# Gram matrices gathered head by head, three output tiles begun early, and the gate's first copy in another pool

## The chip, the cores and the metric

The kernel runs on one core of one Trainium2 chip. The metric is the time of one execution in microseconds (us), as the device reports it; several executions give a median. A core has a matrix engine (TensorE, in the profile PE, with its weight loads as PEld), three engines for element-wise work (VectorE or DVE, ScalarE or ACT, GpSimd or POOL) and SyncE (SP), which here only issues transfers. POOL issues transfers too. Each engine runs its own instructions strictly in order and waits on semaphores for the others. SBUF is the on-chip memory, PSUM the banks into which PE accumulates.

## The reference

One layer of a bidirectional encoder over two groups of 256 tokens (together T = 512 columns), model width 2048, in float32:

```
h = h + W_out [ NA(heads 0..7) ; GatedDeltaNet-bidir(heads 0..7) ]( RMSNorm(h) )
h = h + SwiGLU( RMSNorm(h) )
y = RMSNorm(h)
```

NA is neighbourhood attention on a grid. The gated DeltaNet takes q, k and v through a convolution over five tokens and a SiLU, normalises q and k, and then works in chunks of 64 tokens: for each head, chunk and direction it needs the products of keys with keys and of queries with keys (the Gram matrices), each scaled by decays, the inverse of a unit triangular 64x64 matrix made of them, and a recurrence over the chunks:

```
a_mat = where(strict, (k_beta k^T) * decay, 0)
t_mat = solve_triangular(I + a_mat, I)
u = t_mat v_beta ;  w = t_mat (k_beta * exp(g)) ;  qk = where(tri, (q k^T) * decay, 0)
v_new = u_i - w_i S ;  o = (q_i exp(g_i)) S + qk_i v_new ;  S = S exp(g_last) + (k_i ...)^T v_new
```

## The kernel before

Every large product is done in float32 by splitting each operand into a high part that PE takes at full rate and the rest: hi·hi + lo·hi + hi·lo, three matmuls (`mm3`). A weight tile of 1024x128 comes by one 512-KB transfer on SP (`w_raw`), ACT makes `w_hi` from it and DVE `w_lo` (L128 and L129). Raw, hi and lo have three buffers each. A half tile (`half_gemm`) is 24 such matmuls into a PSUM bank `ps_g` (three banks), a `col_tile` two half tiles, 128 output columns for all tokens.

PE's matmuls keep the order in which the program writes them. Everything else is put in order on its engine when the kernel is built, by a list scheduler with priorities that reckons durations; its result is a fixed row of instructions for each engine. Small jobs are written as generators (`chains`, `side`, `vector_work`) that `pump()` moves on by a step between matmuls, so the constants KQ_GAP, NA_START, LANE_START, CORE_START say after how many steps a job's matmuls or first instructions follow.

The order of the work:

1. The input is split. Then come the key and query tiles of the eight DeltaNet heads, two `col_tile`s a head. Each is evacuated (`ev_xi`), convolved (`conv_silu`: ACT `cacc`, four steps on DVE at L333, ACT `kq` with SiLU at L337; `cacc` has one buffer, `kq` two) and stored to `s_kq` by POOL. ACT squares the queries (`q_sq`, L571) and splits the squares (`sqh`; `sql` on DVE). `kq_post` (L343) follows eight steps later: 8 Gram matmuls of 64 rows and a row of ones against `sqh` and `sql` on PE, in three banks `ps_s`; ACT copies them to SBUF (`gs` L361, `qrow` L369), POOL stores them to the DRAM arrays `s_gram` (four transfers of 64 KB) and `s_qq`. `gs` uses the memory of the attention's `ev_kT` and `ev_vT`. ACT makes the decays (`E`, 22 short instructions a head) in between.
2. The eight attention heads, three `col_tile`s each (q, k, v): `qT`, `ev_kT` and `ev_vT` (L289) evacuate them, then PE transposes `ev_vT`, takes the scores, and so on. Beside them `lanes()` (L455) does the triangular inverses on DVE, all heads, chunks and directions at once, one in each partition. It begins with two transfers of 2 MB on POOL which bring all of `s_gram` into `kkq`, one for each direction, and eight small ones for `qq`. The first DVE instruction that reads them is `nkx` (L472).
3. The value and gate tiles of the DeltaNet and the recurrences (`recur` L691, `finish_head`), whose query operand `qg` is loaded by SP.
4. The output projection: first the 16 tiles' attention half (`w_out[i, 0]`) added to the input in SBUF (`h1`) and stored to `s_h1` by POOL, then the DeltaNet half (`w_out[i, 1]`, from L870 on), with `s_h1` loaded again. The last head's recurrence runs beside the first half. The pools `dr`, `na`, `wk`, `xp` close between the halves, and `st` and `gA` open.
5. The gate and up products in blocks of seven (operands `XC`), the first of which copies its first product with ACT into `p1` (`plus_both`, L916, L917), the down projection and the last norm.

Of the kernel before, what the change touches and what calls it, by code (L numbers as in the profile page):

```python
# [8 lines left out]
F32 = mybir.dt.float32  # L9
# [9 lines left out]
P = 128  # L19
# [19 lines left out]
AHEAD = 120  # L39
NA_START = 5  # L40
NA_GAP = 10
# [3 lines left out]
CORE_START = 2  # L45
CORE_START0 = 6
LANE_START = 4
N_GAP = 1
# [15 lines left out]
def hybrid_encoder(ctx: ExitStack, tc: tile.TileContext, xT, w_in, w_ba, w_out, w_gate,  # L64
# [110 lines left out]
    def pump():  # L175
        advance(chains)
        advance(side)

    def pause(n):
        for _ in range(n):  # L180
            yield

    def half_gemm(ps, src, xs, start, stop, every=2):

        wh, wl = load_w(src, [8, P])
        for k in range(8):
# [154 lines left out]
    na = na_cm.__enter__()  # L341

    def kq_post(h, kq, sqh, sql):  # L343
        yield from pause(KQ_START if h == 0 else KQ_GAP)
# [23 lines left out]
        for pp in range(2):  # L368
            nc.scalar.copy(ranged(qrow[:1], pp), q5[:, :, pp])  # L369
        nc.gpsimd.dma_start(s_qq[h], qrow[:1])  # L370
        if h == H - 1:
            vector_work.append(lanes())

# [81 lines left out]
    def lanes():  # L455
        beta, kd, eg, dg, E = (gt[n] for n in ("beta", "kd", "eg", "dg", "E"))
        qq = vec("qq")
        for d in range(2):
            nc.gpsimd.dma_start(kkq[half[d]].rearrange("p s w c -> p (s w c)"),
                                s_gram.rearrange("k n s w c -> (k n) (s w c)"))  # L460
        for d in range(2):
# [233 lines left out]
    def recur(h, zs):  # L695
        dr = state["dr"]
        while h not in prepared:
            yield
        yield from pause(CORE_START0 if h == 0 else CORE_START)
        uq, kq, vn, kd = prepared[h]  # L700
# [148 lines left out]
    for i in pairs:  # L849
        ps = pg.tile([P, T], F32, tag="g", name="ps_g")  # L850
        half_gemm(ps, w_out[i, 0], nas, True, True, 1)
        hk = h1[i // 8][:, i % 8]
        tt(hk, hk, ps, ALU.add)
        nc.gpsimd.dma_start(s_h1[i], hk)
    while chains or side:
        pump()
    dr_cm.__exit__(None, None, None)
    na_cm.__exit__(None, None, None)
    wk_cm.__exit__(None, None, None)
    xp_cm.__exit__(None, None, None)  # L860
# [6 lines left out]
    gA = ga_cm.__enter__()  # L867
    st_cm = tc.tile_pool(name="st", bufs=1, side="right", reuse_waits="tile")
    st = st_cm.__enter__()
    acc = gA.tile([P, T], F32, tag="acc", name="ssq_acc2")  # L870
    A11, S3, S1, A12, S2, S4, A22 = range(7)
    for n, i in enumerate(pairs):
        j = i % 8
        ps = pg.tile([P, T], F32, tag="g", name="ps_g")
        hk = st.tile([P, T], F32, tag="hk", bufs=2, name="hk")
        nc.sync.dma_start(hk, s_h1[i])
        half_gemm(ps, w_out[i, 1], dns, True, True)
        tt(hk, hk, ps, ALU.add)
        nc.gpsimd.dma_start(s_h2[i], hk)
# [55 lines left out]
    def block(src, f, pool, new_out, opened=None):  # L935
# [61 lines left out]
        a = out.rearrange("p (f b) t -> p f (b t)", f=2)  # L997
        tt(a, a, rstd2[:, None, :].broadcast_to([P, 2, T]), ALU.mult)
        return out

    rstd2 = gA.tile([P, T], F32, tag="rstd2", name="rstd2")

    def token_rstd2():
        ps = sm_tile()
        mm(ps, ones, acc, start=True, stop=True)
        rstd_bcast(ps, rstd2, state["fp"], 1, "p7")

# [216 lines left out]
```

## Time and profile before

| | |
|---|---|
| median of three runs | 2338.06 us (2337.35 to 2338.17) |
| the profiled execution | 2341.7 us |
| its span, first to last instruction | 2339.9 us |
| mean granted clock of TensorE | 0.993 |
| PE busy | 2305.3 us, 99% of the span |
| DVE, ACT, POOL busy | 1614.1, 973.5, 220.5 us |
| moved by the DMA engines | 374.23 MB, mean 160 GB/s |

A row of the profile names the line, the engine, the operation, the tile that it writes and those that it reads, and how often. "Idle before, releaser" is the time that the engine stood still ahead of it and what ended this. Several views are used: what an engine waited for, an engine's timeline, windows of the span with the granted clock, and one tile's instructions.

### The profile page before, as it was taken

How to read it: one execution, taken by the hardware profiler on the slowest of the kernel's cores; microseconds unless marked ns; L12 is line 12 of the kernel's file. 1: busy time of each engine (PE TensorE's matmuls, PEld its weight loads, DVE VectorE, ACT ScalarE, POOL GpSimd, SP SyncE). 2: the span in 40 equal slices, each digit the busy share in tenths (PEclk: the TensorE clock that was granted, in tenths of full speed). 3: DMA queues.
4: the chain of work that ended last, by engine and by line, in shares of the span. 5: the costliest groups of instructions: out<-in, count | busy, mean ns of one | idle time of the engine just before them, and what ended most of it. 6: DMA issues, size and time to landing. Idle time of an engine off the chain costs nothing.

```text
span 2339.9 us, 31301 instructions
## 1 busy us (share of the span) xinstructions
PE 2305.3 (99%) x12092; PEld 1934.0 (83%) x12092; DVE 1614.1 (69%) x2380; ACT 973.5 (42%) x1472; POOL 220.5 (9%) x332
## 2 busy tenths in 40 slices
PE   9999999999999999999999999999999999999998
PEld 7887778887778788888888888888888878888887
DVE  7744699984666536788888888888888753422346
ACT  6777232333333315544444444444444331311125
POOL 2211200011000011101001001010100200000000
PEclk9999999999999999999999999999999999999999
DMA  5434623346434555677777777777776652423231
GB/s 202 133 118 140 156 93 97 102 110 201 128 118 135 198 181 182 198 197 207 198 201 203 198 201 195 208 198 207 195 193 180 216 195 94 135 99 97 92 126 73
DMA packets 105492, 374.23 MB, mean 160 GB/s; under 512 B 13840, under 2 KB 14256, under 8 KB 104192
## 3 DMA queue, kind: packets, MB, share of 16 engines
q1 hardware_dynamic: 75248, 268.74, 34.4%
q0 software_dynamic: 30096, 103.50, 19.7%
q8 instruction: 95, 1.56, 0.3%
q14 instruction: 53, 0.43, 0.1%
HBM read 336.19 MB, written 36.00 MB: 159 GB/s over the span
## 4 chain that ended last, share of the span: by engine, by line
PE 76%; DVE 12%; ACT 4%; DMA 4%; issue 3%; POOL 0%; SPq 0%; DVEq 0%; ACTq 0%; POOLq 0%
PE ps_g L76 28%; PE ps_a L76 11%; PE ps_d L76 10%; PE ps_c L76 10%; PE ps_s L76 10%; PE ps_b L76 5%; DVE w_lo L129 2%; DVE W L544 2%; DMA w_raw<-in_w_in_dram 2%; DVE prod L542 2%; DMA raw_a<-s_act 1%; ACT w_hi L128 1%; DVE cacc L333 1%; PE ps_o L76 1%; ACT E L450 1%
## 5 line engine op out<-in xcount | busy, mean ns | idle before, releaser
L129 DVE TENSOR_TENSOR w_lo<-w_raw,w_hi 128x1024 fp32r<-128x1024 f32 x222 | 271.2, 1222 | 302.2 <-ACT w_hi L128 298.8
L128 ACT ACTIVATE w_hi<-w_raw 128x1024 fp32r<-128x1024 f32 x222 | 234.2, 1057 | 538.1 <-PE ps_s L76 285.8
L76 PE MATMUL ps_g<-xhi,w_hi 128*128 128x512 f32 x896 | 362.2, 404 | 3.7 <-ACT w_hi L128 2.3
L76 PE MATMUL ps_g<-xlo,w_hi 128*128 128x512 f32 x896 | 350.5, 391 | 0.7 <-DVE xlo L237 0.7
L76 PE MATMUL ps_g<-xhi,w_lo 128*128 128x512 f32 x896 | 350.5, 391 | 0.5 <-DVE w_lo L129 0.5
L76 PE MATMUL ps_a<-xc,w_hi 128*128 128x512 f32 x704 | 252.3, 397 | 3.2 <-DVE p L917 2.1
L76 PE MATMUL ps_c<-xc,w_hi 128*128 128x512 f32 x704 | 249.1, 393 | 0.0
L76 PE MATMUL ps_d<-xc,w_hi 128*128 128x512 f32 x704 | 249.1, 393 | 0.0
L128 ACT ACTIVATE w_hi<-w_first 128x1024 fp32r<-128x1024 f32 x132 | 140.1, 1061 | 203.7 <-PE ps_c L76 108.9
L128 ACT ACTIVATE w_hi<-b 128x1024 fp32r<-128x1024 f32 x132 | 140.1, 1062 | 190.2 <-issue 111.5
L129 DVE TENSOR_TENSOR w_lo<-w_first,w_hi 128x1024 fp32r<-128x1024 f32 x132 | 161.6, 1224 | 72.2 <-ACT w_hi L128 68.1
L76 PEld LDWEIGHTS ps_g<-xhi,w_hi 128*128 128x128 f32 x896 | 168.7, 188 | 41.2 <-issue 5.7
L76 PEld LDWEIGHTS ps_g<-xhi,w_lo 128*128 128x128 f32 x896 | 168.6, 188 | 37.6 <-DVE w_lo L129 1.5
L76 PE MATMUL ps_a<-xc,w_lo 128*128 128x256 f32 x704 | 197.9, 281 | 0.0
L76 PEld LDWEIGHTS ps_g<-xlo,w_hi 128*128 128x128 f32 x896 | 169.0, 189 | 34.7 <-DVE xlo L237 1.8
L76 PE MATMUL ps_c<-xc,w_lo 128*128 128x256 f32 x704 | 197.2, 280 | 0.0
L76 PE MATMUL ps_d<-xc,w_lo 128*128 128x256 f32 x704 | 197.1, 280 | 0.0
L129 DVE TENSOR_TENSOR w_lo<-b,w_hi 128x1024 fp32r<-128x1024 f32 x132 | 161.2, 1221 | 7.5 <-ACT w_hi L128 0.9
L76 PEld LDWEIGHTS ps_a<-xc,w_hi 128*128 128x128 f32 x704 | 132.6, 188 | 39.1 <-issue 6.3
L76 PEld LDWEIGHTS ps_c<-xc,w_hi 128*128 128x128 f32 x704 | 131.8, 187 | 30.0
L76 PEld LDWEIGHTS ps_d<-xc,w_hi 128*128 128x128 f32 x704 | 131.8, 187 | 30.0
L76 PEld LDWEIGHTS ps_a<-xc,w_lo 128*128 128x128 f32 x704 | 133.7, 190 | 0.0
(332 smaller groups left out, 4309.2 us busy)
## 6 DMA issues: line engine op xcount, KB each, us to landing
w_raw<-in_w_in_dram SPq DMA_DIRECT2D x110, 512.0 KB, 3.4
w_raw<-in_w_down_dram SPq DMA_DIRECT2D x88, 512.0 KB, 3.4
b<-in_w_gate_dram SPq DMA_DIRECT2D x66, 512.0 KB, 4.1
b<-in_w_up_dram SPq DMA_DIRECT2D x66, 512.0 KB, 5.5
w_raw<-in_w_out_dram SPq DMA_DIRECT2D x32, 512.0 KB, 3.6
w_second<-in_w_gate_dram SPq DMA_DIRECT2D x22, 512.0 KB, 8.4
w_first<-in_w_gate_dram SPq DMA_DIRECT2D x22, 512.0 KB, 6.2
w_second<-in_w_gate_dram POOLq DMA_DIRECT2D x22, 512.0 KB, 5.5
```

What stands on the lines that cost most here:

```text
L76: pin(nc.tensor.matmul(*a, **k))
L128: act(out=hi, in_=src, func=AF.Copy)
L129: tt(lo, src, r32(hi), ALU.subtract)
L333: stt(a3[:, :, lo:hi], x3[:, :, lo + o:hi + o], cw[:, ct, j:j + 1], a3[:, :, lo:hi], ALU.mult, ALU.add)
L450: pin(act(out=E[half[0], s, s:], in_=G[half[0], s:], func=AF.Exp, bias=NG[half[0], s:s + 1]))
L542: tt(pv, W[:, s0:s1, s0:c], kkq[:, c, 0, None, s0:c].broadcast_to([P, n, j]), ALU.mult)
L544: nc.vector.tensor_reduce(W[:, s0:s1, c], pv, AX.X, ALU.add)
```

## The change

It has four parts.

First, the gather. The two 2-MB transfers of `lanes()` are replaced by `gather(h)`: eight transfers on POOL, each of two partitions by 8192 numbers (64 KB), that bring one head's Gram matrices into `kkq`. `kq_post` of head h calls it for head h − 1, behind its own stores, and that of head 7 for head 7 too. The loads of `qq` stay where they were. With it LANE_START goes from 4 to 2, NA_START from 5 to 8, and CORE_START0 (6, the first recurrence's pause) is dropped for CORE_START (2).

Second, three tiles of the projection's second half (EARLY) do seven of their eight steps ahead of the closing of the pools, and the eighth behind it. For the first two of them `h1` is taken from SBUF, not through `s_h1`. `st` opens earlier.

Third, `p1` comes from the pool `gA` in place of `fp`.

Fourth, `rstd2` takes the memory of `acc` in `gA`, which makes room for it.

```diff
-NA_START = 5
+NA_START = 8
...
-CORE_START0 = 6
-LANE_START = 4
+LANE_START = 2
+
+EARLY = 3
...
+    def gather(h):
+
+        for d in range(2):
+            for k in range(4):
+                p0 = d * 64 + k * 16 + h * NB
+                nc.gpsimd.dma_start(kkq[p0:p0 + NB].rearrange("p s w c -> p (s w c)"),
+                                    s_gram[k, h * NB:h * NB + NB].rearrange("n s w c -> n (s w c)"))
...
         nc.gpsimd.dma_start(s_qq[h], qrow[:1])
+        if h:
+            gather(h - 1)
         if h == H - 1:
+            gather(h)
             vector_work.append(lanes())
...
-        for d in range(2):
-            nc.gpsimd.dma_start(kkq[half[d]].rearrange("p s w c -> p (s w c)"),
-                                s_gram.rearrange("k n s w c -> (k n) (s w c)"))
...
-        yield from pause(CORE_START0 if h == 0 else CORE_START)
+        yield from pause(CORE_START)
...
-        nc.gpsimd.dma_start(s_h1[i], hk)
+        if i not in pairs[:2]:
+            nc.gpsimd.dma_start(s_h1[i], hk)
+
+    early = []
+    for i in pairs[:EARLY]:
+        ps = pg.tile([P, T], F32, tag="g", name="ps_g")
+        wh, wl = load_w(w_out[i, 1], [8, P])
+        for k in range(7):
+            while k not in finished:
+                pump()
+            mm3(ps, wh[:, k], wl[:, k], dns[k][0], dns[k][1], k == 0, False)
+            pump()
+        early.append((ps, wh, wl))
     while chains or side:
         pump()
     dr_cm.__exit__(None, None, None)
     na_cm.__exit__(None, None, None)
+    st_cm = tc.tile_pool(name="st", bufs=1, side="right", reuse_waits="tile")
+    st = st_cm.__enter__()
+    hks = []
+    for i, (ps, wh, wl) in zip(pairs[:2], early):
+        mm3(ps, wh[:, 7], wl[:, 7], dns[7][0], dns[7][1], False, True)
+        hk = st.tile([P, T], F32, tag="hk", bufs=2, name="hk")
+        tt(hk, h1[i // 8][:, i % 8], ps, ALU.add)
+        hks.append(hk)
...
-        p1 = fp.tile([P, L], F32, tag="p1", name="p1")
+        p1 = gA.tile([P, L], F32, tag="p1", name="p1")
```

The scheduler builds other rows from this. Three places follow. In the changed kernel the line numbers are one higher from the split on (w_hi L129, w_lo L130), and more further down.

ACT in the stretch of the key and query tiles, before: the weight splits, the table load and the SiLU of head 7's key tile, then of its query tile, the squares and their split.

```order
L128 ACTIVATE w_hi<-w_raw 128x1024
L337 ACT_TABLE_LOAD
L337 ACTIVATE kq<-cacc 128x2x128 x2
L128 ACTIVATE w_hi<-w_raw 128x1024
L327 ACTIVATE cacc<-ev_xi,cw 128x512
L337 ACTIVATE kq<-cacc 128x2x128 x2
L128 ACTIVATE w_hi<-w_raw 128x1024
L571 ACTIVATE q_sq<-kq 128x512
L128 ACTIVATE sqh<-q_sq 128x512
```

The same piece of the changed kernel (head 7; heads 5 and 6 have the same piece, with one `cacc` more):

```order
L129 ACTIVATE w_hi<-w_raw 128x1024 x4
L338 ACT_TABLE_LOAD
L338 ACTIVATE kq<-cacc 128x2x128 x2
L370 COPY gs<-ps_s 128x256 x2
L328 ACTIVATE cacc<-ev_xi,cw 128x512
L378 COPY qrow<-ps_s 1x2x2x64
L378 COPY qrow<-ps_s 1x2x128
L338 ACTIVATE kq<-cacc 128x2x128 x2
L580 ACTIVATE q_sq<-kq 128x512
L129 ACTIVATE sqh<-q_sq 128x512
```

Four weight splits now stand ahead of the table load, and the Gram copies `gs` of the head before have come from ahead of them to behind them.

DVE at the first attention head, before: the weight splits two by two between the evacuations of the key and the value tile.

```order
L129 TENSOR_TENSOR w_lo<-w_raw,w_hi 128x1024 x2
L289 TENSOR_TENSOR ev_kT<-ps_g,rstd 128x512
L129 TENSOR_TENSOR w_lo<-w_raw,w_hi 128x1024 x2
L289 TENSOR_TENSOR ev_vT<-ps_g,rstd 128x512
L129 TENSOR_TENSOR w_lo<-w_raw,w_hi 128x1024 x2
L604 TENSOR_TENSOR na_s<-ps_s,bias 128x512
```

The changed kernel from the end of the key and query tiles on: six splits, the key tile, and then the lanes (`nkx` and what follows).

```order
L647 SCALAR_TENSOR_TENSOR qT<-ps_g,rstd 128x512
L130 TENSOR_TENSOR w_lo<-w_raw,w_hi 128x1024 x6
L290 TENSOR_TENSOR ev_kT<-ps_g,rstd 128x512
L481 TENSOR_SCALAR nkx<-kkq 128x64
L156 TENSOR_SCALAR nw<-nkx 128x64
L512 TENSOR_TENSOR kkq<-kkq,E 128x32x64
```

The piece 28 rows further on, with the evacuation of the value tile in it:

```order
L504 TENSOR_TENSOR Dm<-nkr,rb 128x64
L483 TENSOR_TENSOR nqs<-nqx,nqr 128x64
L290 TENSOR_TENSOR ev_vT<-ps_g,rstd 128x512
L493 TENSOR_SCALAR rqd<-nqr 128x64 x2
L505 TENSOR_SCALAR ndm<-Dm 128x64
```

`ev_vT` stood two weight splits behind `ev_kT`; now 34 instructions of the lanes stand between them, from `nkx` to `nqs`.

SP at the start of the output projection, before: `nml` are the attention outputs, `h_0` and `h_1` the input (512 KB each), `qg` the last head's queries.

```order
L838 DMA nml<-s_na 128x2x512 x4
L136 DMA w_raw<-in_w_out_dram 128x1024
L842 DMA h_1_6601<-in_xT_dram 128x1024
L842 DMA h_0_6600<-in_xT_dram 128x1024 x4
L842 DMA h_1_6601<-in_xT_dram 128x1024 x3
L702 DMA qg<-s_eg 128x2048
```

The changed kernel:

```order
L847 DMA nml<-s_na 128x2x512 x4
L137 DMA w_raw<-in_w_out_dram 128x1024
L711 DMA qg<-s_eg 128x2048
L851 DMA h_0_6697<-in_xT_dram 128x1024 x4
L851 DMA h_1_6698<-in_xT_dram 128x1024 x4
```

`qg` has moved from behind the eight loads to ahead of them.

More of the change, by code (lines that the diff above doesn't have):

```diff
@@ L867, in hybrid_encoder @@
     gA = ga_cm.__enter__()
-    st_cm = tc.tile_pool(name="st", bufs=1, side="right", reuse_waits="tile")
-    st = st_cm.__enter__()
     acc = gA.tile([P, T], F32, tag="acc", name="ssq_acc2")
@@ L873, in hybrid_encoder @@
         j = i % 8
[L874 to L878, printed above, removed]
+        if n < 2:
+            hk = hks[n]
+        else:
+            hk = st.tile([P, T], F32, tag="hk", bufs=2, name="hk")
+            nc.sync.dma_start(hk, s_h1[i])
+            if n < EARLY:
+                ps, wh, wl = early[n]
+                mm3(ps, wh[:, 7], wl[:, 7], dns[7][0], dns[7][1], False, True)
+            else:
+                ps = pg.tile([P, T], F32, tag="g", name="ps_g")
+                half_gemm(ps, w_out[i, 1], dns, True, True)
+            tt(hk, hk, ps, ALU.add)
         nc.gpsimd.dma_start(s_h2[i], hk)
@@ L997, in block @@
         a = out.rearrange("p (f b) t -> p f (b t)", f=2)
-        tt(a, a, rstd2[:, None, :].broadcast_to([P, 2, T]), ALU.mult)
+        tt(a, a, state["rstd2"][:, None, :].broadcast_to([P, 2, T]), ALU.mult)
         return out
-    rstd2 = gA.tile([P, T], F32, tag="rstd2", name="rstd2")
     def token_rstd2():
@@ L1005, in token_rstd2 @@
         mm(ps, ones, acc, start=True, stop=True)
-        rstd_bcast(ps, rstd2, state["fp"], 1, "p7")
+        state["rstd2"] = gA.tile([P, T], F32, tag="acc", name="rstd2")
+        rstd_bcast(ps, state["rstd2"], state["fp"], 1, "p7")
     def open_gate():
```

## The prediction

> **What bounds the kernel now.** The page comes first. It tells which engine fills the span.
>
> ```profile
> span 2339.9 us, 31301 instructions
> PE 2305.3 (99%) x12092; PEld 1934.0 (83%) x12092; DVE 1614.1 (69%) x2380; ACT 973.5 (42%) x1472; POOL 220.5 (9%) x332
> ```
>
> TensorE (PE) works 2305.3 of 2339.9 us. There are some 35 us that it does not fill, and a change that leaves the matmuls as they are can win no more than a part of these. It can lose without limit: anything that makes PE wait goes straight into the time. So the question for each edit is whether a PE wait goes or comes. The second view is what PE waits for, over the whole span (total, times, longest, in us):
>
> ```profile
> PE ps_g L76 <- ACT w_hi L128: 4.1, 2, 2.3
> PE ps_s L76 <- DVE qg L739: 3.1, 1, 3.1
> PE ps_a L76 <- DVE p L917: 2.1, 1, 2.1
> PE ps_s L79 <- DVE ev_vT L289: 1.8, 2, 1.4
> ```
>
> Three of these lie where the change works. The third view is PE's timeline at those places (start, duration, matmul, and in brackets the idle time ahead of it), and the fourth the windows around them (window, its length, busy us of PE, PEld, DVE, ACT and POOL, granted clock, DMA share, GB/s):
>
> ```profile
> 259.45 0.50 PE L76 MATMUL ps_g<-xhi,w_hi 128*128 128x512 f32 x1 [2.27 <-ACT w_hi L128]
> 260.71 0.56 PE L76 MATMUL ps_g<-xhi,w_lo 128*128 128x512 f32 x1 [0.52 <-DVE w_lo L129]
> ```
>
> ```profile
> 257.00:268.00 11.00, 8.20 (x30) 6.09 (x29) 8.54 (x17) 6.33 (x16) 1.06 (x2) 0.84 0.53 173
> 783.00:795.00 12.00, 8.94 (x55) 6.63 (x56) 6.67 (x17) 1.66 (x4) 0.57 (x1) 0.72 0.45 162
> 968.00:988.00 20.00, 17.92 (x89) 14.82 (x88) 15.29 (x19) 11.07 (x16) 3.24 (x4) 0.91 0.82 217
> ```
>
> A PE gap costs more than its idle time: behind each of the three the granted clock drops. 11 us at 0.84 lack 1.8 us, 12 us at 0.72 lack 3.4 us (some of it inside the gap), 20 us at 0.91 lack 1.8 us.
>
> **What the change takes away.** Each gap is priced as idle time plus clock.
>
> The first, at 257 us, has its cause in the old gather: of five weight loads between 228 and 262 us one took 24.3 us to land, because the two 2-MB transfers of kkq held the DMA engines (the tile views of w_raw and of kkq in that stretch, then POOL's timeline):
>
> ```profile
> DMA to landing us min/median/max: 3.3/20.1/24.3
> ```
>
> ```profile
> DMA to landing us min/median/max: 14.2/19.3/24.5
> ```
>
> ```profile
> 233.04 1.05 POOL L459 DMA_DIRECT2D kkq<-s_gram  x2 [4.13 <-DMA s_gram<-gs]
> ```
>
> With the 4 MB cut into 64 pieces over eight heads that burst is gone: 2.27 + 0.52 + 1.8 = 4.5 us. The second, at 785 us, is the last head's query load, which stood behind eight 512-KB loads on SP; the order now has it ahead of them. Its tile's view:
>
> ```profile
> L702 SPq DMA_DIRECT2D qg<-s_eg x1: 326/326/326, 777.1 to 777.1; - x1
> DMA to landing us min/median/max: 8.9/8.9/8.9
> ```
>
>  That gives 3.1 us of idle and 2.4 of the 3.4 of clock: 5.5 us (3.1 to 6.4). The third, at 979 us: p1 took its place in a pool that had to wait for the last reader of the pool before it; in gA it doesn't, and ACT's copy stands ahead of the weight work. 2.1 + 1.8 = 3.8 us. Together 13.8 us.
>
> By the Trainium skill ("TensorE: Matmul & The Clock Gate", section "HAM oscillation — how this bites in real kernels") only idle gaps above some 3.4 us throttle PE; here a gap of 2.08 us was followed by a drop to 0.91 over 20 us, so the row decides; by the rule the three gaps would be worth 7.9 us and the forecast would lie 6 us higher.
>
> **What it moves, and what that costs.** The order of the changed kernel shows more than the diff says. From head 4 on, ACT's stream has the weight splits w_hi in blocks of four, and the silu of both tiles of a head (kq), the Gram copies of the head before (gs) and the convolution's first product (cacc) all behind such a block. Before, they stood one by one between single w_hi. The reason is the gathers: POOL issues eight of them ahead of each head's store of kq, and the scheduler reckons that kq's buffer comes free late. How late it really comes free no longer matters, since ACT runs in order and the fourth w_hi of the block has a wait of its own: three buffers, so it starts when PE has ended the half tile three before. The trace shows this wait, and the length of a half tile (24 matmuls), in the distance of two rows: 238.47 − 233.03 = 5.44 us, 0.227 us for each matmul.
>
> ```profile
> 206.87 1.28 ACT L337 ACT_TABLE_LOAD   x1 [1.73 <-issue]
> 208.16 0.73 ACT L337 ACTIVATE kq<-cacc 128x256 f32<-128x256 f32 x2
> 209.74 0.71 ACT L327 ACTIVATE cacc<-ev_xi,cw 128x512 f32<-128x512 f32 x1
> 214.20 0.72 ACT L337 ACTIVATE kq<-cacc 128x256 f32<-128x256 f32 x2 [3.75 <-DVE cacc L333]
> 215.78 0.61 ACT L571 ACTIVATE q_sq<-kq 128x512 f32<-128x512 f32 x1
> 216.43 0.63 ACT L128 ACTIVATE sqh<-q_sq 128x512 fp32r<-128x512 f32 x1
> 225.33 0.63 ACT L361 COPY gs<-ps_s 128x256 f32<-128x256 f32 x2
> 233.03 1.06 ACT L128 ACTIVATE w_hi<-w_raw 128x1024 fp32r<-128x1024 f32 x1 [4.37 <-PE ps_g L76]
> 238.47 1.06 ACT L128 ACTIVATE w_hi<-w_raw 128x1024 fp32r<-128x1024 f32 x1 [4.38 <-PE ps_g L76]
> ```
>
> ```profile
> 211.01 3.10 DVE L333 SCALAR_TENSOR_TENSOR cacc<-ev_xi,cw,cacc 128x508 f32<-128x508 f32 x4
> 217.09 0.69 DVE L129 TENSOR_TENSOR sql<-q_sq,sqh 128x512 fp32r<-128x512 f32 x1
> 232.50 0.69 DVE L289 TENSOR_TENSOR ev_kT<-ps_g,rstd 128x512 f32<-128x512 f32 x1 [3.82 <-DMA s_gram<-gs]
> ```
>
> Heads 5, 6 and 7. Let T be the end on PE of the half tile for which the block's last w_hi waits. From there the chain is w_hi 1.06, table 1.28, k's kq 0.73, gs 0.63, q's cacc 0.71, four DVE steps 3.10, q's kq 0.72: 8.2 us. PE's order puts this head's Gram matmuls six matmuls into the next half tile, 6 × 0.227 = 1.4 us behind T. So PE stands still for 6.8 us. Then come the two row matmuls: 0.61 + 0.71 + 0.63 = 1.95 us to sqh and 2.8 to sql against some 1.1 us of Gram matmuls and a row matmul between, so 1.3 us more; before, the two rows took 0.5:
>
> ```profile
> 215.84 1.09 PE L76 MATMUL ps_s<-kq 128*64 128x128 f32 x16
> 217.11 0.39 PE L76 MATMUL ps_s<-sqh,ones_r 128*1 128x512 f32 x1 [0.18 <-ACT sqh L128]
> 217.83 0.40 PE L76 MATMUL ps_s<-sql,ones_r 128*1 128x512 f32 x1 [0.34 <-DVE sql L129]
> ```
>
> That is 6.8 + 1.3 − 0.5 = 7.6 us of idle for a head. The clock behind it I put between the 1.8 and the 3.4 us of the windows, at 2.4: 10 us a head, 30 us for three (23 without any clock, 33 with the whole). Head 4 only finds its PSUM buffers late, since gs of head 3 stands behind a w_hi: 1.5 us (0 to 3).
>
> The first attention head. Now DVE has six w_lo in one piece ahead of ev_kT, the evacuation of its k tile, and ACT six w_hi ahead of gs of head 7. PE needs the k tile's PSUM bank when it has ended the half tile for which the sixth w_hi waits: call that U. gs ends at U + 1.06 + 0.63 = U + 1.7. ev_kT takes gs's place in memory and so waits for the stores of s_gram; before, it started 232.50 − 225.96 = 6.5 us behind the end of gs. That makes U + 8.2, and U + 8.9 for its end: 8.9 us of idle where there was none, and 1 us of clock, as little work follows before the next wait: 9.9 us.
>
> That next wait is for ev_vT. In DVE's order 34 operations of the lanes have moved ahead of it, beginning with nkx, which needs all the gathers. POOL issues s_gram from U + 1.7:
>
> ```profile
> 225.98 2.42 POOL L363 DMA_DIRECT2D s_gram<-gs  x4 [10.18 <-ACT gs L361]
> 228.40 0.51 POOL L370 DMA_DIRECT2D s_qq<-qrow  x1
> 234.08 2.88 POOL L464 DMA_DIRECT2D qq<-s_qq  x6
> 247.50 0.48 POOL L464 DMA_DIRECT2D qq<-s_qq  x1 [10.54 <-DMA kkq<-s_gram]
> ```
>
> 2.42 + 0.51 bring it to U + 4.6, and 16 gathers follow at 1.05 / 2 = 0.53. The last two rows show that a ninth transfer (here behind two of kkq and six of qq) waits for the landing of the first, so the second eight wait for the first eight. For the landing of a 64-KB gather there is no row; the nearest is that of s_gram's tile, whose stores have the same bytes:
>
> ```profile
> DMA to landing us min/median/max: 2.1/4.8/24.5
> ```
>
> (This row is of tile s_gram and counts the two big ones as well.) With its 4.8 us: first eight landed from U + 9.9, second eight issued by U + 14.1, all landed at U + 18.9. The bounds: 16 us if no landing holds the issue and one 32-KB row takes 24.5 / 8 = 3.1 us (the old gather's 128 rows over 16 engines), and 54 us if all rows go through the same two engines (16 × 3.1 behind U + 4.6). I take 19.
>
> ```profile
> 262.49 0.21 DVE L472 TENSOR_SCALAR nkx<-kkq 128x64 f32<-128x64 f32 x1
> 265.68 1.22 DVE L129 TENSOR_TENSOR w_lo<-w_raw,w_hi 128x1024 fp32r<-128x1024 f32 x1
> 274.71 0.23 DVE L474 TENSOR_TENSOR nqs<-nqx,nqr 128x64 f32<-128x64 f32 x1
> ```
>
> From nkx to the end of nqs before: 12.4 us, with two w_lo (2.4) and about 1 us of attention steps inside that now stand elsewhere, and without one product of some 1 us that now stands here: 10 us. (The eight loads of qq stand behind the gathers on POOL, each behind the landing of the eighth transfer ahead of it, and would land some 5 us after the gathers; DVE asks for them, at nqx, some 5 us after nkx, so that costs nothing, or a us or two.) With 0.69 for itself ev_vT ends at U + 29.7. PE reaches its transposes six matmuls behind U + 8.9, at U + 10.3: 19.4 us idle, and 2.4 of clock: 21.8 us. Behind that I see no further PE wait: the next weight split stands some 12 us of DVE work later, and PE has two half tiles in hand.
>
> Early tiles of the output projection: head 7 is finished when they begin, so nothing waits for it, but all three weight buffers stay taken until each tile's last matmuls, so the fourth tile's w_hi (1.06) starts at the first tile's end, and its w_lo (1.22) follows when DVE has made two additions of 0.69: 1.4 + 1.2 = 2.6 us against eight matmuls, 1.8 us, so 1 us (0 to 3). The rest (SBUF copies of two tiles, rstd2 in acc's place, the earlier recurrence) lies beside PE work of 5.44 us a half tile and costs nothing; if that cover failed, it would be a DVE step of 0.69 us.
>
> **The sum.** Lost: 30 + 1.5 + 9.9 + 21.8 + 1 = 64. Won: 13.8. Net +50. The profiled execution took 2341.7 us, so 2392 by its own time; the median lies 3.6 us lower, so 2388.
>
> **Rivals.** (a) The other side: the stalls don't come, since the rows moved behind the blocks are done before PE asks. The deciding point is the cover of 1.4 us against a chain of 8.2; for it speaks only that ACT is 42% busy over the span, against it the row of w_hi released by PE. Then only the gaps go: 2338 − 14 = 2324. It would turn at stalls of 14 us in all.
> (b) The gathers fall on few DMA engines. Then nkx comes up to 35 us later (54 − 19): 2423; with four engines about half of it, 2400. For it speaks that two partitions are two rows; against it nothing in the profile, which has no such transfer. The Trainium skill ("DMA: Bandwidth & Descriptors", section "Why a DMA increments its semaphore by 16 and not by 1") lets such a GpSimd transfer use two engines, taken in turn by a cursor, which would speak against this rival; no run here shows it yet.
> (c) The stalls come, but at their lower ends: 23 for the three heads, none for head 4, 8.9, and 16.4 for the vT wait, no clock: 48 − 14 = +34, 2372.
> (d) The stalls and the gains balance: within 0.2% (4.7 us, about what a measurement of this kernel can tell from no change), 2338.
>
> Chances: forecast 0.57, (b) 0.15, (c) 0.13, (a) 0.12, (d) 0.03. Faster 0.12, same 0.03, slower 0.85. The range leaves out (a), (d) and a little of each end: 2352, some 20 us under (c), which a smaller vT wait alone would give, to 2424, the end of (b).
>
> **What would show it.** PE's timeline between 150 and 240 us with three waits of 6 to 8 us ahead of ps_s<-kq; then one of some 9 us ahead of ps_g, released by ev_kT, and one of some 19 us ahead of ps_s<-ident,ev_vT; no gap ahead of S,qg near the output projection and of ps_a near the gate's start; granted clock below 1 behind each stall. The forecast is wrong if PE has no gap over 3 us in that stretch, or if a gap of tens of us has a weight load (DMA) as its releaser.

## The result, and the profile after

The changed kernel takes 2403.7 us in the median (2402.7 to 2406.3, six runs) where the kernel before, run beside it, takes 2338.1 us (2337.3 to 2340.5, six runs). The ratio is 1.028 (1.0267 to 1.0293): 65.6 us slower. In the two profiled executions the span grew from 2339.9 to 2400.9 us, by 61.0. The page of the changed kernel begins:

```profile
span 2400.9 us, 31348 instructions
PE 2306.8 (96%) x12092; PEld 1934.7 (81%) x12092; DVE 1616.0 (67%) x2380; ACT 977.6 (41%) x1474; POOL 250.2 (10%) x392
PEclk9998879999999999999999999999999999999999
```

PE is busy as long as before (2306.8 against 2305.3 us) and does as many matmuls, so the 61 us are waiting. The row of clocks says where: slices 4 to 6, 180 to 360 us, the key and query tiles and the first attention head. PE's waits in the changed kernel (total, times, longest, in us):

```profile
PE ps_s L80 <- DVE ev_vT L290: 34.6, 1, 34.6
PE ps_s L77 <- ACT kq L338: 20.6, 3, 7.8
PE ps_s L77 <- ACT gs L370: 10.1, 1, 10.1
PE ps_g L77 <- DVE ev_kT L290: 7.0, 1, 7.0
...
PE ps_a L77 <- DVE p L951: 1.2, 1, 1.2
...
PE ps_d L77 <- ACT w_hi L129: 1.1, 1, 1.1
...
PE ps_g L77 <- DVE w_lo L130: 0.8, 1, 0.8
```

Six single waits are new and large. PE's timeline puts them in order (start, duration, matmul, idle time ahead of it and releaser): heads 4 to 7, then the first attention head's key and value tiles.

```profile
154.88 1.33 PE L77 MATMUL ps_s<-kq 128*64 128x128 f32 x10 [10.11 <-ACT gs L370]
...
187.62 1.12 PE L77 MATMUL ps_s<-kq 128*64 128x128 f32 x8 [7.80 <-ACT kq L338]
...
219.93 1.34 PE L77 MATMUL ps_s<-kq 128*64 128x128 f32 x10 [6.40 <-ACT kq L338]
...
253.09 1.32 PE L77 MATMUL ps_s<-kq 128*64 128x128 f32 x9 [6.39 <-ACT kq L338]
...
294.96 0.79 PE L77 MATMUL ps_g<-xhi,w_hi 128*128 128x512 f32 x1 [7.03 <-DVE ev_kT L290]
...
332.47 0.87 PE L80 MATMUL ps_s<-ident,ev_vT 128*128 128x128 f32 x3 [34.59 <-DVE ev_vT L290]
```

Together they are 72.3 us. They pull the clock down too, as the windows around one stall of a head, the long wait and the matmuls behind it show:

```profile
212.00:228.00 16.00, 9.20 (x40) 6.63 (x39) 8.42 (x11) 13.01 (x30) 7.47 (x14) 0.68 0.32 97
...
301.50:335.70 34.20, 3.23 (x10) 2.81 (x11) 14.16 (x42) 0.58 (x1) 11.88 (x24) 0.50 0.08 28
335.70:345.00 9.30, 9.30 (x42) 7.69 (x42) 9.19 (x12) 3.94 (x11) 1.43 (x2) 1.00 0.12 31
```

The matmuls that ran at half clock behind the six waits lost 12.4 us (half of 3.3, 4.7, 6.5, 4.0, 3.1 and 3.2 us). The account against before: lost 72.3 + 0.8 (the early tile's w_lo) + 12.4 = 85.5; gone are 13.6 us of smaller idle times and 9.6 of clock behind four of them, 23.2. That makes 62.3, where 61.0 were measured.

What went, and what of it stayed away: the gap of 2.27 + 0.52 us at 259 us (4.5 with its clock); the 3.06 at 788 us (5.9 with clock); of 2.08 at 981 us two gaps of 1.10 and 1.20 are left, without a drop of the clock (1.5); three gaps of 1.59, 1.38 and 0.87 around 310, 446 and 544 us (3.8); and one in the down projection, 1.81 + 0.72 at 1905 us (5.9 with clock).

### The profile page after: what moved, and what is told of

The parts are those of the page before. It is cut to its first block, busy times and chain, and to the rows that moved or that the text cites. A ratio compares the mean times of both kernels' runs of the same rounds, so it can differ in the third digit from the quotient of the medians.

```text
span 2400.9 us, 31348 instructions
## 1 busy us (share of the span) xinstructions
PE 2306.8 (96%) x12092; PEld 1934.7 (81%) x12092; DVE 1616.0 (67%) x2380; ACT 977.6 (41%) x1474; POOL 250.2 (10%) x392
## 4 chain that ended last, share of the span: by engine, by line
PE 89%; DVE 4%; ACT 3%; DMA 2%; issue 1%; SPq 0%; POOL 0%; DVEq 0%; ACTq 0%
PE ps_g L77 39%; PE ps_s L77 12%; PE ps_a L77 10%; PE ps_c L77 10%; PE ps_d L77 10%; PE ps_b L77 5%; DVE cacc L334 1%; PE ps_o L77 1%; DMA kkq<-s_gram 1%; PE ps_s L80 1%; DVE w_lo L130 1%; DMA w_raw<-in_w_in_dram 1%; ACT w_hi L129 1%; ACT E L462 0%; ACT E L464 0%
## 5 line engine op out<-in xcount | busy, mean ns | idle before, releaser
L130 DVE TENSOR_TENSOR w_lo<-w_raw,w_hi 128x1024 fp32r<-128x1024 f32 x222 | 271.1, 1222 | 309.4 <-ACT w_hi L129 306.1
L129 ACT ACTIVATE w_hi<-w_raw 128x1024 fp32r<-128x1024 f32 x222 | 234.4, 1057 | 579.3 <-PE ps_s L77 280.7
L129 ACT ACTIVATE w_hi<-w_first 128x1024 fp32r<-128x1024 f32 x132 | 140.1, 1061 | 204.3 <-PE ps_c L77 109.2
L129 ACT ACTIVATE w_hi<-b 128x1024 fp32r<-128x1024 f32 x132 | 140.2, 1062 | 193.0 <-issue 115.4
L130 DVE TENSOR_TENSOR w_lo<-w_first,w_hi 128x1024 fp32r<-128x1024 f32 x132 | 161.7, 1225 | 75.0 <-ACT w_hi L129 70.9
L130 DVE TENSOR_TENSOR w_lo<-b,w_hi 128x1024 fp32r<-128x1024 f32 x132 | 161.2, 1221 | 7.7 <-ACT w_hi L129 0.8
```

The lines of the kernel that those rows point to most:

```text
L129: act(out=hi, in_=src, func=AF.Copy)
L130: tt(lo, src, r32(hi), ALU.subtract)
```

## The experiments

Two theories stood at the start. **A**: there are two causes. The gathers ahead of each store of `kq` in POOL's queue make the scheduler build the blocks on ACT and DVE, and with them the waits at heads 4 to 7 and at `ev_kT`; LANE_START = 2 puts the lanes ahead of `ev_vT`, and with it the sixth wait. **B**: the gathers' slow landing is the cause of the waits, the constants do little. The later runs ask how much of each wait is a loss of its own. Every kernel computes the whole layer. Medians, with before beside it on the same chip:

| run | kernel | us | before | ratio (95%) |
|---|---|---|---|---|
| e1 | gathers alone | 2395.1 | 2336.4 | 1.025 (1.0233–1.0267) |
| e2 | LANE_START 2 alone | 2351.9 | 2336.4 | 1.0068 (1.0053–1.0083) |
| e3 | changed, LANE_START 4 | 2391.7 | 2336.4 | 1.0236 (1.0221–1.0251) |
| e4 | early tiles, p1, rstd2 alone | 2337.5 | 2336.4 | 1.0006 (0.9996–1.0015) |
| e5 | gathers alone, on SP | 2397.0 | 2334.6 | 1.026 (1.0246–1.0274) |
| e6 | gathers alone, in two halves | 2377.3 | 2334.6 | 1.0178 (1.0164–1.0192) |
| e7 | changed, one-row gathers | 2404.2 | 2334.6 | 1.0293 (1.0279–1.0307) |
| e8 | CORE_START0 2, p1 alone | 2336.2 | 2334.6 | 1.0002 (0.9993–1.0011) |
| e9 | e1, stores on SP | 2356.9 | 2338.0 | 1.0076 (1.0063–1.0089) |
| e10 | changed, stores on SP | 2350.0 | 2338.0 | 1.0049 (1.0034–1.0065) |
| e11 | e10, LANE_START 4 | 2350.0 | 2338.0 | 1.0043 (1.003–1.0056) |
| e12 | e9, CORE_START0 2, p1 | 2359.5 | 2338.0 | 1.0086 (1.0073–1.0099) |

### Gathers alone (e1_gather_only)

The kernel before with the gather part of the change, the constants as before.

```diff
         nc.gpsimd.dma_start(s_qq[h], qrow[:1])
+        if h:
+            gather(h - 1)
         if h == H - 1:
+            gather(h)
             vector_work.append(lanes())
```

> The kernel before, with the new gathers alone (all constants, the early tiles and p1 as before). Theory A (order): the loss comes from where the gathers on POOL make the scheduler put the SiLU, the Gram copies and ev_kT behind blocks of weight splits; the wait for ev_vT does not come from the gathers but from LANE_START, which has its old value here. So the four waits ahead of ps_s<-kq stay (10.1 + 7.8 + 6.4 + 6.4 us and some 8 us of clock), one wait of 7 to 10 us at the first attention head stays, the 34.6 us wait goes, and the old gap at 257 us (4.5 us) goes: about 2380 us. Theory B (transfers): the loss comes from the gathers themselves, slow and late, and the whole of it stays, the ev_vT wait too: about 2415 us.

It took 2395 us, between the 2380 of A and the 2415 of B. PE's waits:

```profile
PE ps_s L76 <- ACT kq L337: 19.2, 3, 6.4
PE ps_s L76 <- ACT gs L369: 10.1, 1, 10.1
PE ps_s L76 <- DMA uq<-s_uq: 9.4, 2, 8.7
PE ps_s L79 <- DVE ev_vT L289: 7.4, 2, 7.1
PE ps_g L76 <- DVE ev_kT L289: 7.2, 1, 7.2
```

The four waits at the heads and one at an evacuation are there with nothing but the gathers: that half of A holds. The wait of 34.6 us is not there, as A has it. But two waits stand in its place that A did not have: 7.2 us for a second `ev_kT`, which now stands behind the lanes, and 8.7 us at the first recurrence, far later, for `uq`, which the lanes make.

### LANE_START alone (e2_lanes2)

```diff
-LANE_START = 4
+LANE_START = 2
```

> The kernel before with one digit changed, LANE_START 2 for 4; gathers, early tiles and p1 as before. Theory A (order): DVE's row now has the lanes' first 34 instructions ahead of ev_vT, although no transfer is changed. nkx waits for the 2-MB gathers (landed at 258 us), ev_vT ends some 11 us later at 269, PE is at its transposes at about 247: one wait of 20 to 23 us ahead of ps_s<-ident,ev_vT and 2 to 3 us of clock, while the gap at 257 us goes: about 2357 us. Theory B (transfers): no change, 2338 us.

One line of the kernel before gives the wait, with the old two transfers of 2 MB:

```profile
270.55 0.66 PE L79 MATMUL ps_s<-ident,ev_vT 128*128 128x128 f32 x2 [23.33 <-DVE ev_vT L289]
```

The mechanism of A is shown: the constant alone puts `nkx` ahead of `ev_vT`. PE was 25.4 us behind before's matmuls there, but 17.8 at 310 us and some 13 at 600 us: part of it was given back, since before's gaps at 259, 310, 446 and 544 us do not come in this kernel or are smaller.

### The changed kernel with LANE_START 4 (e3_after_lanes4)

```diff
-LANE_START = 2
+LANE_START = 4
```

> The changed kernel with LANE_START back at 4, everything else as changed. Theory A (order): ev_vT stands right behind ev_kT, the wait of 34.6 us goes with its clock, the other five waits stay: about 2367 us. Theory B (transfers): the gathers land as late as before, so the lanes and all that hangs on them stay late: about 2400 us.

It is 55 us slower than before where the changed kernel is 66 slower: only some 10 us came back, where A expected 36. The wait of 34.6 us went, and others came:

```profile
PE ps_g L77 <- DVE ev_kT L290: 10.9, 2, 7.2
...
PE ps_s L77 <- DMA uq<-s_uq: 7.7, 1, 7.7
```

The second is at 607.6 us, ahead of the first recurrence. The lanes have two due times. They take some 240 us of DVE (from `nkx` to the last product, table below), and the recurrence asks for their result at 557 to 626 us. If `nkx` comes late, PE waits early (with the lanes put ahead) or late (without). From the rows of DVE and PE in the traces, in us:

| | nkx starts | last product of the lanes | first matmul with `uq` | PE's wait for it |
|---|---|---|---|---|
| before | 262.5 | 502.4 | 557.3 | none |
| changed | 321.4 | 556.9 | 626.2 | none |
| e1 | 327.1 | 566.5 | 613.2 | 8.7 |
| e3 | 323.7 | 561.3 | 607.6 | 7.7 |
| e9 | 283.3 | 522.7 | 568.7 | 8.0 + 3.4 |
| e10 | 263.4 | 498.9 | 568.3 | none |
| e11 | 280.3 | 517.8 | 565.1 | 10.3 + 2.7 |

### The other parts alone (e4_rest)

The changed kernel with the old gathers and constants; its three other parts stay. The core of what it has beyond before:

```diff
+    for i in pairs[:EARLY]:
+        ps = pg.tile([P, T], F32, tag="g", name="ps_g")
+        wh, wl = load_w(w_out[i, 1], [8, P])
...
-        p1 = fp.tile([P, L], F32, tag="p1", name="p1")
+        p1 = gA.tile([P, L], F32, tag="p1", name="p1")
...
+        state["rstd2"] = gA.tile([P, T], F32, tag="acc", name="rstd2")
```

> The changed kernel with the two 2-MB gathers and the three old constants put back: only the early tiles, p1 in gA and rstd2 in acc's place are left of the change. Both theories have the same place for the loss (gone); the run tells what the other parts are worth. If the gaps at 785, 979 and 1905 us of the kernel before went because of these parts: 6 + 1 + 6.4 - 1.1 of the early tiles, about 2326 us. Rival: the 1905 gap went only because everything came at another moment: about 2332 us.

No change that can be measured; both forecasts, 2326 and 2332 us, were too low. The gap at the gate's start is 1.10 + 1.21 us in place of 2.08, an early tile waits 0.79 us, and the gap in the down projection is gone; but PE drifts 2.9 us behind before through the gate and up products without a single gap that explains it, which takes more than half of this back. And the wait for `qg` stays:

```profile
789.09 1.13 PE L78 MATMUL ps_s<-S,qg 128*64 128x128 f32 x8 [5.55 <-DVE qg L749]
```

So its going in the changed kernel is owed to none of these parts.

### CORE_START0 and p1 alone (e8_core2_p1)

```diff
-CORE_START0 = 6
+CORE_START0 = 2
...
-        p1 = fp.tile([P, L], F32, tag="p1", name="p1")
+        p1 = gA.tile([P, L], F32, tag="p1", name="p1")
...
+        state["rstd2"] = gA.tile([P, T], F32, tag="acc", name="rstd2")
```

> The kernel before with two small parts of the change: the first recurrence's pause 2 (CORE_START0 dropped), and p1 in gA with rstd2 in acc's place. Old gathers, no early tiles, the other constants old. Theory: the last head's query load stands ahead of the eight input loads in SP's row again, so the gap at 785 us and its clock go (6 us), and the gap at 979 us gives 1 us: about 2329 us. Rival: the waits come back later, as the gap at 1905 us of the kernel before went and came with drift in the gate stage: 2336 us, no change.

The wait for `qg` went, but the recurrence, begun earlier, now waits for the lanes:

```profile
PE ps_s L76 <- DMA uq<-s_uq: 5.3, 2, 4.0
```

Net nothing (1.0002), as the rival had it. In the changed kernel this wait doesn't come because PE is 69 us late there, while the lanes are 54 us late (table above).

### Gathers on SP (e5_gather_sp)

```diff
-                nc.gpsimd.dma_start(kkq[p0:p0 + NB].rearrange("p s w c -> p (s w c)"),
+                nc.sync.dma_start(kkq[p0:p0 + NB].rearrange("p s w c -> p (s w c)"),
```

> The kernel before with the new gathers alone, as in the run of the gathers alone, but issued by SP in place of POOL. The transfers are the same 64 of two partitions; the stores of the Gram copies and of kq no longer stand behind them in POOL's queue. Theory A (order): ACT's row has each head's Gram copies and SiLU ahead of the weight blocks again, so the four waits ahead of ps_s<-kq and the one ahead of ps_s<-ident,ev_vT (37 us with their clock) go; the last gathers are issued earlier and the lanes are in time: 2334 to 2342 us. Theory B (transfers): 32-KB rows on two DMA engines hold up stores and weight loads whoever issues them: the waits stay, about 2390 us.

Theory A missed by 55 us or more. Theory B came near with its 2390 us, but not by its mechanism: with the gathers out of POOL's queue there is no wait for `kq` or `gs` of a head, as the theory of the order has it. But SP issues in order, too: a gather that waits for the store of `s_gram` holds all weight loads behind it. First PE's waits, then SP's:

```profile
PE ps_g L76 <- ACT w_hi L128: 54.4, 10, 23.8
```

```profile
SPq L348 <- DMA s_gram<-gs: 88.8, 11, 22.9
```

### Stores on SP, gathers on POOL (e9_stores_sp)

e1 with the short stores of `kq_post` and of `kq` moved instead:

```diff
-                nc.gpsimd.dma_start(
+                nc.sync.dma_start(
                     s_gram[2 * hf:2 * hf + 2, h * NB + b].rearrange("k s w c -> s k (w c)"),
...
-        nc.gpsimd.dma_start(s_qq[h], qrow[:1])
+        nc.sync.dma_start(s_qq[h], qrow[:1])
...
-        nc.gpsimd.dma_start(s_kq[h], kq)
+        nc.sync.dma_start(s_kq[h], kq)
```

> The kernel before with the new gathers on POOL, as in the run of the gathers alone, but the three stores of each head (kq, the Gram copies, the row of squares) issued by SP, so that they no longer stand behind gathers. ACT's and DVE's rows come out word for word as in the kernel before. Theory A (order, caused by stores behind gathers in one queue): the four waits ahead of ps_s<-kq, the one for ev_vT and the one for ev_kT go, and with the 2-MB transfers the gap at 257 us: 2330 to 2336 us. Theory B (the two-engine transfers themselves do harm): about 2375 us or more. A third way: SP's weight loads wait behind stores as they did behind gathers, some us each head: up to 2350 us.

This tells the two explanations of the heads' waits apart: the gathers are on POOL as in e1 and move as many bytes, but no store that frees a buffer stands behind them. Up to 260 us the rows of ACT and DVE are the same as those of before. The window from 100 to 260 us (PE busy, PEld, DVE, ACT, POOL, clock, DMA share, GB/s) in before, in e1 and in e9:

```profile
100.00:260.00 160.00, 156.69 (x745) 126.71 (x743) 70.30 (x83) 101.86 (x218) 25.36 (x45) 1.00 0.48 142
```

```profile
100.00:260.00 160.00, 129.89 (x587) 103.84 (x586) 64.56 (x76) 95.68 (x207) 39.10 (x74) 0.88 0.35 111
```

```profile
100.00:260.00 160.00, 155.82 (x739) 125.42 (x738) 69.74 (x83) 101.69 (x218) 30.59 (x62) 1.00 0.45 139
```

PE does 745, 587 and 739 matmuls in it. The four waits and their drop of the clock come with the queue, not with the traffic. That it is the built row that holds PE, and not a store that lands late, is read from ACT's timeline (head 6, below), where no wait is for a transfer; no kernel here has the queue of e1 with the rows of before. All three forecasts of the total missed, though: what is left of e9's 19 us stands behind that window. The last gathers are issued only at 239 us (POOL waited 23.80 us for the stores) and have landed by 262.1 us, 4 us later than the two big transfers of before. But `nkx` starts 20.8 us later than before, and it does not wait for a transfer. From DVE's timeline in e9:

```profile
282.18 1.22 DVE L129 TENSOR_TENSOR w_lo<-w_raw,w_hi 128x1024 fp32r<-128x1024 f32 x1 [5.99 <-ACT w_hi L128]
283.32 0.21 DVE L480 TENSOR_SCALAR nkx<-kkq 128x64 f32<-128x64 f32 x1
```

Behind 261 us DVE's row is no longer that of before: between `ev_vT` and `nkx` stand seven weight splits, where before has two, and most of them wait for their `w_hi`. So this too is for the most part a matter of the built order and not of the landing. In PE's waits it shows as 11.4 us at the recurrence and 5.4 at the second head's `ev_kT`, which stands behind `nkx`.

### The changed kernel with stores on SP (e10_all_stores_sp, e11_all_stores_sp_lanes4)

The same edit in the changed kernel, and then with LANE_START 4 as well.

> The whole change with the three stores of each head issued by SP. The blocks in ACT's row are gone, but LANE_START 2 still has 34 lane instructions ahead of ev_vT on DVE. Theory A: no waits ahead of ps_s<-kq; the last gathers land at about 250 us, the six weight splits ahead of nkx end at 254, ev_vT at 265, PE is at its transposes at 253: a wait of some 12 us and 2 us of clock, less the gaps at 257 and 785 us: about 2341 us. If the landing and not the order makes the ev_vT wait, it shrinks to a few us: 2330 us.

> The run before, with LANE_START back at 4, so that ev_vT stands behind two weight splits as in the kernel before; gathers head by head, NA_START 8, CORE_START 2, early tiles and p1 as changed. Theory A: none of the waits up to 300 us is left, the gap at 257 us goes, that at 785 us goes: 2325 to 2332 us. Rival: as with the two small parts alone, what goes in one place comes back in another (the recurrence's first wait, the gate stage): 2336 us, no change.

e10 takes 53.7 us off the changed kernel, and is still 9 us above its forecast. One large wait is left:

```profile
274.49 0.87 PE L80 MATMUL ps_s<-ident,ev_vT 128*128 128x128 f32 x3 [18.92 <-DVE ev_vT L290]
```

and e11, which takes it away, is no faster, where 2325 to 2336 us were forecast:

```profile
565.06 0.77 PE L77 MATMUL ps_s<-dvn,uq 128*128 128x128 f32 x2 [10.28 <-DMA uq<-s_uq]
```

With two smaller ones (2.68 behind it, 3.70 at `ev_kT`) that is 16.7 us in place of 18.9. So the sixth wait is for the most part a place, not a price of its own: with the lanes ahead of `ev_vT` PE waits early, with the lanes behind it PE waits late. What makes them late differs. In the changed kernel and in e3 it is the landing (last gather 321.3 and 323.2 us, `nkx` 321.4 and 323.7). In e10 and e11 the last gather has landed by 260.3 us; e10 starts `nkx` 3 us behind that, e11 only at 280.3, behind seven weight splits as in e9. Whether gathers head by head with `nkx` at the landing and `ev_vT` ahead of it would pay neither wait, no run shows.

### Stores on SP, CORE_START0 and p1 (e12_stores_sp_core2_p1)

e9 with the edit of e8, tried as a version that might beat both.

> The kernel before with the gathers on POOL, the stores on SP, the first recurrence's pause 2, and p1 in gA; old NA_START and LANE_START, no early tiles. Theory A: gaps at 257, 785 and part of that at 979 us go; the recurrence's first wait (5.3 us at 554 us with the two small parts alone) goes too if the lanes start earlier, since their last gathers land earlier than the 2-MB ones did: about 2326 us. Rival: the lanes don't start earlier, the wait stays: 2334 us.

It does not: 2359.5 us, with `nkx` at 285.4 us and 10.9 us of waits at the recurrence for `uq`. Both forecasts, 2326 and 2334 us, missed. None of the twelve kernels is faster than before.

### Other shapes of the gather (e6_halves, e7_one_row)

e6: before with the gather in two pieces of eight partitions a transfer (16 in all), behind the stores of heads 4 and 7 (the first cut is against e1). e7: the changed kernel with one partition a transfer (128 in all).

```diff
-        if h:
-            gather(h - 1)
+        if h == 4:
+            gather(0)
         if h == H - 1:
-            gather(h)
+            gather(4)
...
-                nc.gpsimd.dma_start(kkq[p0:p0 + NB].rearrange("p s w c -> p (s w c)"),
+                nc.gpsimd.dma_start(kkq[p0:p0 + 8].rearrange("p s w c -> p (s w c)"),
```

```diff
+                for b in range(NB):
+                    p0 = d * 64 + k * 16 + h * NB + b
+                    nc.gpsimd.dma_start(kkq[p0:p0 + 1].rearrange("p s w c -> p (s w c)"),
```

> The kernel before with the gather in two halves of four heads each, 8 partitions (256 KB) a transfer, 16 transfers on POOL, the first eight behind head 4, the others behind head 7. Theory A (order): only head 7's SiLU stands behind a block of four weight splits, so one wait of 6.4 us ahead of ps_s<-kq with 1.6 us of clock; the gap at 257 us shrinks by half: about 2341 us. On the transfers: if the number of partitions sets the number of DMA engines, the second eight take 8 rows on each of 8 engines, 10 to 18 us; if such transfers use two engines whatever their size, 32 rows on each, over 40 us, and the lanes and the recurrences come late by some 25 us: about 2360 us.

> The changed kernel with each gather of two partitions cut into two of one partition (32 KB), 128 transfers. The order in the key and query stretch keeps its blocks for heads 5 to 7 and so its waits. What differs is the landing of the last 32 rows. If a transfer's rows go to as many engines as it has partitions, always the same, then all 32 rows go through one engine: 32 x 1.3 = 42 us, the wait for ev_vT grows from 34.6 to about 50 us: about 2418 us. If one-row transfers are spread over the engines, issue sets the pace, 32 x 0.5 = 16 us, and the wait falls to about 25 us: about 2394 us.

e6 (2377 us) has one wait for `kq` in place of three, but two for late weights (11.6 and 8.3 us) and 7.9 us at the recurrence; both of its forecasts, 2341 and 2360 us, were too low. e7 (2404 us) is as slow as the changed kernel, with 38.1 us at `ev_vT`, between its two forecasts of 25 and 50: its last 32 transfers land in 7.3 us in the median, but POOL waits on landings of gathers 28.5 us in all. How the gathers land in the changed kernel, from its window of 309 to 321 us and the tile view of `kkq`, and in e6 from 258 to 286 us:

```profile
q0 software_dynamic: 312, 0.58, 12.5%
...
kkq<-s_gram POOLq DMA_DIRECT2D x3, 64.0 KB, 9.6
```

```profile
DMA to landing us min/median/max: 4.4/10.2/18.1
```

```profile
q0 software_dynamic: 193, 1.59, 41.9%
```

12.5% of 16 engines is two engines' work, while several transfers of two rows are outstanding: in the packets exactly two rows of 32 KB are under way for 23.0 of 24.3 us, each 1.2 to 2.3 us long, one starting when another ends. With eight partitions a transfer it is eight rows, some 3.9 us each. The prediction's rival (b) was right in the count of engines, not in the price that it put to a row (3.1 us; 1.5 measured in the mean).

## Why the prediction was right or wrong

**What bounds the kernel.** Right: PE's work did not change, and all of the difference is PE's waiting and the clock behind it.

**Heads 5, 6 and 7.** Forecast 6.8 us of idle each from the chain of 8.2 us behind a block's last w_hi; measured 7.80, 6.40 and 6.39. ACT's timeline for head 6 shows the chain as it was worked out: w_hi released by PE, table load, `kq` of the keys, `gs`, `cacc`, and `kq` of the queries after DVE's steps.

```profile
211.99 1.06 ACT L129 ACTIVATE w_hi<-w_raw 128x1024 fp32r<-128x1024 f32 x1 [4.38 <-PE ps_g L77]
213.07 1.28 ACT L338 ACT_TABLE_LOAD   x1
214.36 0.72 ACT L338 ACTIVATE kq<-cacc 128x256 f32<-128x256 f32 x2
214.99 0.62 ACT L370 COPY gs<-ps_s 128x256 f32<-128x256 f32 x2
215.50 0.73 ACT L328 ACTIVATE cacc<-ev_xi,cw 128x512 f32<-128x512 f32 x1
...
219.46 0.72 ACT L338 ACTIVATE kq<-cacc 128x256 f32<-128x256 f32 x2 [2.73 <-DVE cacc L334]
```

Head 5's block started on a late weight load, which gives its 7.80. The further 1.3 us for the two row matmuls did not come, and the clock cost 7.6 us for the three heads (7.2 forecast). 28.2 us against 30.

**Head 4.** Mis-sized: 1.5 us forecast, 10.1 of idle and 1.7 of clock measured. The step that failed is "gs of head 3 stands behind a w_hi". It stands behind a w_hi that itself stands behind the decays, 22 instructions and a table load. ACT's timeline:

```profile
142.05 1.04 ACT L129 ACTIVATE w_hi<-w_raw 128x1024 fp32r<-128x1024 f32 x1
...
144.30 1.28 ACT L462 ACT_TABLE_LOAD   x1
...
152.56 0.32 ACT L464 ACTIVATE E<-G,NG 64x33 f32<-64x33 f32 x1
152.90 1.06 ACT L129 ACTIVATE w_hi<-w_raw 128x1024 fp32r<-128x1024 f32 x1
...
154.48 0.62 ACT L370 COPY gs<-ps_s 128x256 f32<-128x256 f32 x2
```

From 144.30 to 152.90 ACT does nothing else: 8.6 us. The prediction read what moved behind the weight splits and not what else stands between them.

**The key tile of the first attention head.** 8.9 us of idle forecast, 7.03 measured; 9.9 against 8.6 with the clock. U was 287.7 us in the changed kernel, and `ev_kT` ended at 294.9, U + 7.2.

**The value tile.** 19.4 us forecast, 34.6 measured. The place and the releaser were right, and so were POOL's first gather at U + 4.6 and the 10 us from `nkx` to `ev_vT` (321.38 to 331.65). The landing failed: U + 19 was forecast, from the 4.8 us of a store of the same bytes, and U + 33.6 came, inside the stated bounds of 16 and 54. DVE's timeline, then the chain that ended last in this stretch:

```profile
294.21 0.69 DVE L290 TENSOR_TENSOR ev_kT<-ps_g,rstd 128x512 f32<-128x512 f32 x1 [4.16 <-DMA s_gram<-gs]
321.38 0.22 DVE L481 TENSOR_SCALAR nkx<-kkq 128x64 f32<-128x64 f32 x1 [26.47 <-DMA kkq<-s_gram]
...
331.65 0.67 DVE L290 TENSOR_TENSOR ev_vT<-ps_g,rstd 128x512 f32<-128x512 f32 x1
```

```profile
291.16 5.56 DMA s_gram<-gs
...
297.49 13.98 DMA kkq<-s_gram
...
311.75 9.51 DMA kkq<-s_gram
```

The first gathers also waited for the last stores to land (to 296.7 us), and the two rounds of gathers took 14.0 and 9.5 us, not 4.8 each. Rival (b) had this cause, at too high a price.

**What it gives back.** Not foreseen, and it pulls the other way: the wait is not all loss. The prediction priced `ev_vT` as an addition to the rest. e3 and e11 show that without it PE waits ahead of the recurrence, as the lanes take some 240 us from `nkx` on wherever they stand.

**What was won.** The gap at 257 us went as forecast (4.5). The wait for `qg` went (5.9 against 5.5), but not by itself: e4 keeps it and e8 loses it and pays at the recurrence. The gate's start gave 1.5 and not 3.8: two waits of 1.1 and 1.2 us stood behind the one that the prediction took away whole. Some 10 us in five smaller gaps went that the prediction did not name, 5.9 of them in the down projection; e1 and e4 have the same win, so that no one part of the change owns it, and whether it is a chance of the profiled execution of before stays open; so does the cause of a drift of 2.9 us ahead of it in e4. Early tiles: 1 us forecast, 0.8 and no drop of the clock.

**The sum.** Forecast +50; in the spans +61.0 came (+65.6 in the medians, since the profiled run of before lay 3.6 us above its median and that of the changed kernel 1.0 below). The losses were put too low by 10 at head 4 and by 14 at `ev_vT` and too high by 3 at the others, and the gains too low by 9. So the waits came where and why the prediction said, but that the total came no worse is in part luck: the 9 of the gains and the 3 made up for half of the 24 that were missing. Rival (a), that the stalls don't come, fell: the cover of 1.4 us against a chain of 8.2 decided as the rows said.

## What to carry to other kernels

Where a scheduler builds each engine's row, a transfer put on a queue ahead of a store that frees a buffer can reorder engines that it never touches: here 64 gathers in the queue of the stores left PE 158 matmuls behind at 260 us (587 against 745 from 100 us on, e1), and the same gathers with the stores on another queue 6 (739, e9). The order also decides what a transfer that lands in time is worth: in e9 the first reader stood 21 us behind the landing, behind other work of its engine. When pricing a moved instruction, read everything that stands between it and its new neighbours, and when a wait seems removable, look for the next time at which the same late work is due. Splitting a transfer into pieces of few partitions made it slower to the last byte: with two partitions a piece two rows moved at once, with eight up to eight.

## What the runs showed of the hardware

The granted clock changes on a fixed grid. All half-clock stretches of the traces of before and of the changed kernel inside the span last 3.41 us or a multiple of it (3.41, 6.83, 10.24, 34.1; only the last of each trace is cut by the end), and so do the stretches at full clock between them (23.89 between the heads' stalls). The Trainium skill ("TensorE: Matmul & The Clock Gate", section "Part 1: The HAM clock gate") states a free-running window of 3413 ns, which agrees; that only gaps above some 3.4 us throttle does not agree with these runs: gaps of 2.08 and 3.06 us were each followed by a stretch of half clock, those of 1.1 to 1.6 us by none, and one of 2.10 us in e10 by none either, so the place of a gap on the grid counts beside its length. Laid on the grid, the fourteen traces agree on what counts, the idle time of PE within one window of 3.41 us: each full-clock window with more than 1.9 us of it was followed by a half-clock window, none with less than 1.6 was, and between the two values both occur. Full clock came back behind each half-clock window with less than 0.39 us of it, and behind none with more than 0.49. The 3.06 us ahead of the last head's `qg` put 1.79 us into one window, the 2.10 us in e10 only 1.66. A gap behind which the clock falls therefore costs half of what is left of one or two windows, here 1.6 to 3.3 us, whether the gap was 2 or 35 us long.

Outstanding transfers of two partitions on POOL's queue did not spread: two rows under way at any time, with the queue at 12.5% of 16 engines; on SP's queue (e5) two rows for 47.9 of the 51.7 us in which rows of 32 KB moved. The Trainium skill ("DMA: Bandwidth & Descriptors", section "Why a DMA increments its semaphore by 16 and not by 1") gives such a transfer two engines, which agrees; the cursor that it describes, which moves on from transfer to transfer, would let several run side by side, and that the changed kernel's packets do not show.
